# One layer-pair step of a hybrid recurrent decoder on one Trainium2 core: where the small weights and the mask table lie in SBUF, and when they are loaded

## The chip, the cores and the metric

The kernel runs on one core of one Trainium2 chip. The metric is the device time of one launch in microseconds (us), the median over several runs. The engines are TensorE (PE, with its weight loads PEld), VectorE (DVE), ScalarE (ACT), GpSimd (POOL) and SyncE (SP), which issues nearly all DMA transfers in the order of its queue.

## What is computed

A trunk of two layers runs over 592 tokens at once: 16 meta tokens, 8 sample sequences of 8 tokens and a prompt of 512. The width is 1024. Layer 0 ("even") has Mamba-2 SSD heads beside RG-LRU blocks, layer 1 ("odd") has GLA heads beside HGRN2 heads. Cut to what matters:

```python
for layer in range(2):
    mixed = _even_mixer(h, ...) if layer == 0 else _odd_mixer(h, ...)
    h = _layer_norm(ALPHA * h + mixed, ln1_g[layer], ln1_b[layer])
    h = _layer_norm(ALPHA * h + square(relu(h @ w1[layer])) @ w2[layer], ln2_g[layer], ln2_b[layer])

# even mixer: one narrow input (dt, 16 columns) beside the wide ones
z, xbc, dt_raw, rg_gate, rg_x = jnp.split(h @ w_in_even, EVEN_SPLIT, -1)
# odd mixer: one narrow input (lrg, 16 columns) beside the wide ones
qg, kg, vg, gg, lrg, qh, fh, ih, gh = jnp.split(h @ w_in_odd, ODD_SPLIT, -1)
```

The two narrow inputs, `dt_raw` and `lrg`, are the "small" products: 1024 x 16 weights each.

## The kernel before

**Tiling.** Tokens lie along the free dimension, features on 128 partitions; an activation is 8 tiles H[0..7] of 128 x 592. Each fp32 value is held as two fp32r parts (high and remainder), so that a product of a 1024 x 128 weight unit takes 8 x 3 matmuls for each half of the tokens (296 columns a half). The line of these matmuls is L183; L196 holds the mlp's products, L260 the small product of the even mixer, and L324 the products in `together`, where several outputs take turns over k = 0..7, so that the matmuls of k need H[k] alone.

**Weights.** Units of 512 KB come in the order of use: `load_unit` (L121, SP, three buffers), then `parts` makes the two parts on ACT (L127) and DVE (L128) into one of five buffers.

**The small weights and the masks.** `masks(stack, layer)` opens a pool at the start of each mixer, loads the mask table `msk` (128 x 1122, L103), then the small weights (L106), and splits those on ACT and DVE (L107, L108) into `wsr`. SP reads its queue in order, so the load at L106 stands behind that at L103.

**Places in SBUF.** Pools are stacked: a pool that is opened takes the space that the closed ones before it left, and each of its tiles waits for the readers and writers of those old tiles that it lies over. Worked out from the tile shapes in the order of the pools (a pool's first tile takes the lowest slot, the next ones go down from the top), the masks of the first mixer lie over the tiles of the first loads of x and over the scratch of `softplus` and of the gate table (L411 to L422); the masks of the second mixer lie over the tiles rs[0] and rs[7] of the first layer's mlp.

**Start.** `prep_to(1)`, the first half of x, `prep_to(2)`, the vector table `vec`, the second half of x (L365, split at L347 and L348). The first products are `conv[0]`, the small product and `conv[1]`, each for the first half and then for the second (`by_half`).

**Between the layers.** The first mlp ends with the products of w2 for the second half, the norm's sums (L508, L510), and `finishing`, which makes H for the next layer in L539 (DVE), L540 (ACT) and L541 (DVE). After that POOL adds the bias to rs[0..7] (L756) and writes them to DRAM with its own DMAs (L757, `keep`), as the residual of the next layer. The odd mixer starts with `together(ts[:4], 0)`: the small product, q, k and v0 for the first half; then v1; then the second half. An output is copied out of PSUM (L1510 for the small product, L1495 for q, k and v) into a tile of the pool `go`; there are five PSUM buffers for products.

**Order.** A planner lays down each engine's order of instructions at build time from its own estimates of when operands are ready, earlier lines of the program first; on the chip each engine then keeps that order.

Of the kernel before, what the change touches and what calls it, by code (L numbers as in the profile page):

```python
# [8 lines left out]
F32 = mybir.dt.float32  # L9
F32R = mybir.dt.float32r  # L10
I32 = mybir.dt.int32
AF = mybir.ActivationFunctionType
OP = mybir.AluOpType

P = 128
D = 1024
KT = 8
# [23 lines left out]
FULL = ((0, CS), (CS, T))  # L41
# [7 lines left out]
VEC = {}  # L49
_n = 0  # L50
for _name, _w in (("cw", 80), ("cb", 20), ("ssdg", 8), ("dskip", 8), ("ba", 8), ("bx", 8), ("lam", 8),
# [2 lines left out]
    VEC[_name] = _n  # L54
    _n += _w
NVEC = _n

MSK = {}
_n = 0
# [4 lines left out]
NMSK = _n  # L64
# [7 lines left out]
def _trunk(ctx, tc, nc, I, O):  # L72
    V, A, G, PE = nc.vector, nc.scalar, nc.gpsimd, nc.tensor

    def pool(name, bufs=1, stack=ctx, **k):
        return stack.enter_context(tc.tile_pool(name=name, bufs=bufs, reuse_waits="tile", **k))

    const = pool("const")
# [9 lines left out]
    def px():  # L88
        return pxp.tile([P, 512], F32, tag="px", name="px")

    vec = const.tile([P, NVEC], F32, name="vec")
    row = const.tile([P, 32], F32, name="row")
    ones = const.tile([P, P], F32, name="ones")

    def vc(name, i=0, n=1):
        o = VEC[name] + i
        return vec[:, o:o + n]

    def masks(stack, layer):

        sp = pool("mskp", stack=stack)
        t = sp.tile([P, NMSK], F32, name="msk")
        nc.sync.dma_start(t, I["msk"])  # L103
        small = sp.tile([P, KT, 32], F32R, name="wsr")
        r = sp.tile([P, KT, 16], F32, name="wsm")
        nc.sync.dma_start(r, I["wsm"][:, layer])  # L106
        A.copy(small[:, :, 0:16], r)  # L107
        V.tensor_tensor(small[:, :, 16:32], r, small[:, :, 0:16].bitcast(F32), OP.subtract)  # L108
        return lambda name: small if name == "small" else t[:, slice(*MSK[name])]

# [52 lines left out]
    def prep_to(n):  # L165
        while state["next"] < min(n, len(items)):
            u = state["next"]
            state["next"] += 1
            prepped[u] = items[u]()
# [164 lines left out]
    def run(tasks, by_half=False, after=None):  # L334
        if by_half:
            for i in range(2):
                for t in tasks:
                    t.half(i)
                if after:
                    after(i)  # L340
        else:
            for t in tasks:
                t.half(0)
                t.half(1)
# [8 lines left out]
    def new_h():  # L353
        return [act_tile(hp, "h") for _ in range(KT)]


    H = new_h()
    prep_to(1)
    with ExitStack() as st:
        xt = pool("xp", KT, stack=st)  # L360
        xs = [xt.tile([P, T], F32, tag="xt", name="xt") for _ in range(KT)]

        def load(c0, c1):
            for k in range(KT):
                nc.sync.dma_start(xs[k][:, c0:c1], I["x"][:, k, c0:c1])  # L365
                split(H[k], xs[k], c0, c1)

        load(*FULL[0])
        prep_to(2)
        nc.sync.dma_start(vec, I["vec"])  # L370
        load(*FULL[1])
    nc.sync.dma_start(row, I["row"])
    G.memset(ones, 1.0)

# [14 lines left out]
        G.tensor_scalar(m, x, 0.0, None, OP.max)  # L389
        V.scalar_tensor_tensor(out, t, 2.0, m, OP.mult, OP.add)  # L390

    hcw = const.tile([P, 48], F32, name="hcw")
    hcb = const.tile([P, 12], F32, name="hcb")
    hb = const.tile([P, 16], F32, name="hb")
    sp4 = const.tile([P, 8], F32, name="sp4")
    hg = const.tile([P, 3], F32, name="hg")
    lbt = const.tile([P, 3, 8], F32, name="lbt")
    nlam = const.tile([P, 8], F32, name="nlam")
    V.tensor_scalar(hcw, vc("cw", 0, 48), 0.5, None, OP.mult)
    V.tensor_scalar(hcb, vc("cb", 0, 12), 0.5, None, OP.mult)  # L400
    V.tensor_scalar(hb, vc("ba", 0, 16), 0.5, None, OP.mult)
# [143 lines left out]
    def out_proj(g, ys, close, res, halves, layer):  # L545

        c0, c1 = halves[0][0], halves[1][1]
        out = [None]
        with ExitStack() as st:
            rs, m1, m2 = {}, new_h(), []  # L550
            for k in range(KT):
                split(m1[k], ys[k], c0, c1)

            def first(j):
                rs[j] = g("r")
                nc.sync.dma_start(rs[j][:, c0:c1], res[:, j, c0:c1])

                def f(p, a, b, i):
                    V.scalar_tensor_tensor(rs[j][:, a:b], rs[j][:, a:b], ALPHA, p, OP.mult, OP.add)
                return Task(m1, halves, f)  # L560

            def second(j):
                def f(p, a, b, i):
                    V.tensor_tensor(rs[j][:, a:b], rs[j][:, a:b], p, OP.add)  # L564
                    if j >= KS:
                        norm.add(j, i)
                return Task(m2, halves, f)

            def after(i):
                if out[0] is None:  # L570
                    out[0] = new_h()
                norm.finish(i, out[0])

            for j in range(KT):
                run([first(j)])
                if j == JW:
                    drain()
                    close()
                    ap = pool("oact", KT, stack=st)
                if j >= JW:  # L580
                    while len(m2) < min(KT, (j - JW + 1) * -(-KT // (KT - JW))):
                        k = len(m2)
                        m2.append(act_tile(ap, "m2"))
                        split(m2[k], ys[KT + k], c0, c1)
            norm = Norm(g, rs, halves, "ln1g", "ln1b", layer)
            run([second(j) for j in range(KS)])
            norm.shift()
            run([second(j) for j in range(KS, KT)], by_half=True, after=after)
        return out[0]


    def mlp(H, layer, halves, last, keep=None):

# [4 lines left out]
        with ExitStack() as st:  # L598
# [26 lines left out]
            def operands(i):  # L625

                for k in (i, i + 4):
                    h = H[k][:, :, c0:c1].bitcast(F32)
                    V.tensor_tensor(rs[k][:, c0:c1], h[:, 0], h[:, 1], OP.add)
# [9 lines left out]
            def last_operand(i):  # L639

                t2 = turned[i][:, :, 2, :n].bitcast(F32)
                b21 = H[i + 4][:, :, lo].bitcast(F32)
                t4 = H[i][:, :, hi]
                x = stage()[:, 0, :n]
# [145 lines left out]
    def even_mixer(H, g, mk):  # L790
        ident, umask, lsmask, uxmask, lxmask, seqm, sel, blk = (
            mk(n) for n in ("ident", "u", "ls", "ux", "lx", "seq", "sel", "blk"))
        st = ExitStack()
        cp = pool("cp", 2, stack=st)
        sm = pool("sm", 1, stack=st)
# [319 lines left out]
        ys = [None] * 16  # L1115
        conv = []
        for i, key in ((8, ("B", 0)), (10, ("C", 0)), (9, ("B", 1)), (11, ("C", 1))):
            grp[key] = g("bc")
            conv.append(ssd_conv(i, grp[key], lambda: None))
        run([conv[0], Task(H, FULL, dt_consume, small=mk("small")), conv[1]], by_half=True)  # L1120
        run(conv[2:3])
        active.append(group(0))
        run(conv[3:4])
# [121 lines left out]

    def odd_mixer(H, g, mk):
        ident, umask, lsmask, uxmask, lxmask, seqm, sel, blk = (
            mk(n) for n in ("ident", "u", "ls", "ux", "lx", "seq", "sel", "blk"))  # L1250
        st = ExitStack()
        sm = pool("osm", 1, stack=st)
        sd = pool("osd", 1, stack=st)
        wg2 = sm.tile([32, 512], F32, name="wg2")
        nc.sync.dma_start(wg2, I["wg2"])
        rmask = sm.tile([P, T], F32, name="rmask")
# [248 lines left out]
        ys = []  # L1505
# [23 lines left out]
        for h in range(4):  # L1529
            q, k, v0, v1 = (g(n) for n in ("q", "k", "v", "v"))  # L1530
            tasks = [copy_task(q, TAIL), copy_task(k, FULL), copy_task(v0, FULL), copy_task(v1, FULL)]
            if h == 0:
                ts = [Task(H, FULL, lr_consume, small=mk("small"))] + tasks
                together(ts[:4], 0)
                ts[4].half(0)
                together(ts[:2], 1)
                together(ts[2:4], 1)
                ts[4].half(1)
            else:
                run(tasks)  # L1540
            z = [g("zs"), g("zs")]
            while len(lsg) <= h:
                weave()
            active.append(attend(q, k, lsg[h], 1.0 / 16, P ** -0.5, (v0, v1), z, hg[:, 0:2],
                                 I["gst"][h], O["gla_s"][h], O["gla_p"][h], 1))
            run([silu_task(z[0]), silu_task(z[1])])
# [17 lines left out]
        for h in range(8):  # L1564
# [4 lines left out]
            ls, k = fk[h]  # L1569
# [5 lines left out]
        return ys, st.close  # L1575

    with ExitStack() as st:
        mk = masks(st, 0)
        gp = pool("ge", NGE, stack=st)

        def g(name="g"):
            return gp.tile([P, T], F32, tag="g", name=name)

        ys, close = even_mixer(H, g, mk)
        H = out_proj(g, ys, close, I["x"], FULL, 0)
    res = tc.dram_tile([P, KT, T], F32, name="res")
    H = mlp(H, 0, FULL, False, keep=res)
    with ExitStack() as st:
        mk = masks(st, 1)
        gp = pool("go", NGO, stack=st)  # L1590

        def g(name="g"):
            return gp.tile([P, T], F32, tag="g", name=name)

        ys, close = odd_mixer(H, g, mk)
        ln_set.append(True)
        H = out_proj(g, ys, close, res, EVEN_TAIL, 1)
    mlp(H, 1, EVEN_TAIL, True)
# [157 lines left out]
```

## Time and profile before

| | us |
|---|---|
| median of 3 runs | 1940.32 (1939.97 to 1941.08) |
| the profiled execution | 1940.13 |
| its span | 1938.4 |
| PE busy | 1820.5 |
| DVE, ACT, POOL busy | 1411.8, 1020.7, 370.2 |

The span runs from the first to the last instruction; 1.7 us of the profiled execution's time lie around it. "Busy" is the sum over an engine's instructions. Times in the views are microseconds from the start of the span. The chain of waits goes back from the last instruction, at each step to what released it.

### The profile page before, as it was taken

To read this page: it belongs to the slowest core of one execution; us is meant where nothing else is said; L and a number is where in the kernel's file an instruction comes from. 1 tells how busy PE (TensorE), PEld (TensorE's weight loads), DVE (VectorE), ACT (ScalarE), POOL (GpSimd) and SP (SyncE) were. 2 spreads that over 40 slices of the span, in tenths; PEclk is the share of its full clock that TensorE was granted. 3 is DMA by queue.
4 is the path that set the end of the run, shared out by engine and by line. 5 is a ranking of instruction groups with operands and counts; after the bars stand their busy time and mean duration, and the time that the engine had idled before them with its cause. 6 is when DMAs were issued, how large, how long until landed. Compare 5 with 4: busy or idle time off the path is not lost.

```text
span 1938.4 us, 33527 instructions
## 1 busy us (share of the span) xinstructions
PE 1820.5 (94%) x13534; PEld 1766.0 (91%) x13534; DVE 1411.8 (73%) x2332; ACT 1020.7 (53%) x1903; POOL 370.2 (19%) x403
## 2 busy tenths in 40 slices
PE   4999999999999999992999999999999899999997
PEld 4998999898999999991899999999999899999996
DVE  4767766868999898866345557656565999989868
ACT  3656556623646474623354456566552464646443
POOL 0222232215100000256012222212111400000025
PEclk7999999999999999996899999999999999999998
DMA  5232321421122322313123232332332113232221
GB/s 191 71 109 72 108 96 50 133 89 55 57 71 91 99 87 88 109 66 136 57 101 112 101 101 78 100 102 89 101 127 77 55 55 99 77 109 80 95 98 49
DMA packets 69050, 176.53 MB, mean 91 GB/s; under 512 B 6656, under 2 KB 30464, under 8 KB 67744
## 3 DMA queue, kind: packets, MB, share of 16 engines
q1 hardware_dynamic: 68256, 171.97, 27.1%
q8 instruction: 106, 1.74, 0.4%
q0 software_dynamic: 640, 2.43, 0.3%
q14 instruction: 48, 0.39, 0.1%
HBM read 155.12 MB, written 19.25 MB: 90 GB/s over the span
## 4 chain that ended last, share of the span: by engine, by line
PE 68%; DVE 17%; ACT 6%; issue 4%; POOL 2%; DMA 2%; SPq 0%; ACTq 0%; DVEq 0%; POOLq 0%
PE pm L183 37%; PE pm L196 18%; PE pm L324 3%; DVE w L128 3%; ACT w L127 2%; DVE r L523 1%; POOL sq L675 1%; DVE r L459 1%; PE px L1455 1%; DVE h L541 1%; DVE r L539 1%; POOL r L756 1%; ACT sq L671 1%; DVE acc L824 1%; PE px L1466 1%
## 5 line engine op out<-in xcount | busy, mean ns | idle before, releaser
L183 PE MATMUL pm<-h,w 128*128 128x296 f32 (+2 forms) x5424 | 790.6, 302 | 6.4 <-ACT h L347 5.8
L183 PEld LDWEIGHTS pm<-h,w 128*128 128x128 f32 x5424 | 746.8, 189 | 16.7 <-ACT h L347 5.8
L128 DVE TENSOR_TENSOR w<-raw,w 128x1024 fp32r<-128x1024 f32 x348 | 412.1, 1186 | 136.5 <-ACT w L127 134.6
L127 ACT CAST w<-raw 128x1024 fp32r<-128x1024 f32 x348 | 342.8, 989 | 311.6 <-PE pm L183 110.6
L196 PE MATMUL pm<-ff,w 128*128 128x296 f32 (+1 forms) x2016 | 285.1, 299 | 6.3 <-ACT w L127 3.1
L196 PEld LDWEIGHTS pm<-ff,w 128*128 128x128 f32 x2016 | 273.7, 188 | 15.6 <-ACT w L127 5.5
L196 PE MATMUL pm<-h,w 128*128 128x296 f32 (+1 forms) x1152 | 166.1, 298 | 1.8 <-DVE sq L724 0.9
L196 PEld LDWEIGHTS pm<-h,w 128*128 128x128 f32 x1152 | 158.0, 188 | 4.6 <-ACT sq L727 2.4
L675 POOL TENSOR_TENSOR sq<-sq 128x296 f32<-128x296 f32 (+1 forms) x32 | 27.7, 866 | 636.5 <-ACT ff L674 634.4
L196 PE MATMUL pm<-t,w 128*128 128x296 f32 (+1 forms) x864 | 124.5, 297 | 1.0 <-ACT sq L727 0.7
L196 PEld LDWEIGHTS pm<-t,w 128*128 128x128 f32 x864 | 118.5, 188 | 1.7 <-ACT sq L727 1.2
L183 PE MATMUL pm<-ff,w 128*128 128x296 f32 (+1 forms) x768 | 105.9, 298 | 0.9 <-DVE ff L676 0.9
L183 PEld LDWEIGHTS pm<-ff,w 128*128 128x128 f32 x768 | 103.7, 188 | 2.1 <-DVE ff L676 1.4
L183 PE MATMUL pm<-m,w 128*128 128x296 f32 (+1 forms) x768 | 105.2, 298 | 0.0
L183 PEld LDWEIGHTS pm<-m,w 128*128 128x128 f32 x768 | 103.9, 188 | 0.4
L324 PE MATMUL pm<-h,w 128*128 128x296 f32 (+1 forms) x528 | 81.7, 311 | 9.4 <-DVE r L564 6.7
L324 PEld LDWEIGHTS pm<-h,w 128*128 128x128 f32 x528 | 77.0, 198 | 12.2 <-ACT h L540 7.3
L736 DVE TENSOR_TENSOR r<-r,pm 128x296 f32<-128x296 f32 (+1 forms) x168 | 74.9, 452 | 11.2 <-PE pm L196 10.5
L622 ACT CAST ff<-sq 128x296 fp32r<-128x296 f32 (+5 forms) x96 | 58.0, 618 | 24.4 <-DVE sq L692 11.6
L623 DVE TENSOR_TENSOR ff<-sq,ff 128x296 fp32r<-128x296 f32 (+5 forms) x96 | 64.4, 685 | 5.1 <-ACT ff L622 4.5
L1490 POOL TENSOR_TENSOR o<-o,zs 128x576 f32<-128x576 f32 x16 | 30.8, 1935 | 151.7 <-DVE o L1489 151.7
L1409 POOL TENSOR_TENSOR sin<-sin,ebl 128x1024 f32<-128x1024 f32 (+1 forms) x12 | 31.2, 2600 | 97.9 <-issue 93.2
(410 smaller groups left out, 2502.1 us busy)
## 6 DMA issues: line engine op xcount, KB each, us to landing
raw<-in_w_dram SPq DMA_DIRECT2D x252, 512.0 KB, 3.7
sin<-in_sst_dram SPq DMA_DIRECT2D x8, 512.0 KB, 3.8
out_ssd_s_dram<-sin SPq DMA_DIRECT2D x8, 512.0 KB, 3.6
sin<-in_gst_dram SPq DMA_DIRECT2D x4, 1024.0 KB, 5.8
out_gla_s_dram<-sin SPq DMA_DIRECT2D x4, 1024.0 KB, 3.9
sin<-in_hst_dram SPq DMA_DIRECT2D x8, 512.0 KB, 4.6
out_hgrn_s_dram<-sin SPq DMA_DIRECT2D x8, 512.0 KB, 3.5
xt<-in_x_dram SPq DMA_DIRECT2D x16, 148.0 KB, 3.7
```

The source lines that it names most:

```text
L127: A.copy(w[:, 0, :n], r)
L128: V.tensor_tensor(w[:, 1, :n], r, w[:, 0, :n].bitcast(F32), OP.subtract)
L183: PE.matmul(p[:, :n], w[:, a, ks], xs[k][:, b, c0:c1], start=(k == 0 and i == 0), stop=(k == KT - 1 and i == 2))
L196: PE.matmul(p[:, :n], w[:, a, ks], xs[k][:, b, :n], start=(first and k == 0 and i == 0), stop=(k == 3 and i == 2), skip_group_check=True)
L324: PE.matmul(o[:, :c1 - c0], w, t.xs[k][:, b, c0:c1], start=(k == 0 and j == 0), stop=(k == KT - 1 and j == len(ops) - 1))
L459: V.tensor_tensor(rs[k][:, c0:c1], rs[k][:, c0:c1], c[:, c0:c1], OP.subtract)
L622: A.copy(t[:, 0], x)
L623: V.tensor_tensor(t[:, 1], x, t[:, 0].bitcast(F32), OP.subtract)
L675: G.tensor_tensor(x, x, x, OP.mult)
L736: return lambda p: V.tensor_tensor(y, y, p, op)
L1409: G.tensor_tensor(sin, sin, ebl[:, 0:8].unsqueeze(2).to_broadcast([P, 8, N]), OP.mult)
L1490: G.tensor_tensor(o[v][:, c], o[v][:, c], gate[v][:, c], OP.mult)
```

## The change

The small weights of both mixers are loaded in one transfer (`wsm`, 128 KB) right after the first half of x and split at once: the even mixer's into `wse`, the odd mixer's into `wsr`, which is moved to the pool that lives for the whole kernel. A new pool `evc` is opened ahead of x and closed after the even mixer: it holds `wse`, the first mixer's masks, the columns of the vector table that only the even mixer reads, `row` and five small tables. So those tiles have space of their own, and the load of the first mixer's masks is written right behind the second half of x. The vector table is loaded in two pieces. The odd mixer's masks are now loaded in `odd_mixer` into its pool `osm`, behind the 26 tiles of `go`; the pool `mskp` is gone, and `go` starts 6 KB lower.

```diff
--- before.py
+++ after.py
@@ -54,6 +54,7 @@
     VEC[_name] = _n
     _n += _w
 NVEC = _n
+NEVEN = VEC["ln1g"]
 
 MSK = {}
 _n = 0
@@ -88,25 +89,19 @@
     def px():
         return pxp.tile([P, 512], F32, tag="px", name="px")
 
-    vec = const.tile([P, NVEC], F32, name="vec")
-    row = const.tile([P, 32], F32, name="row")
+    vec = const.tile([P, NVEC - NEVEN], F32, name="vec")
+    wsr = const.tile([P, KT, 32], F32R, name="wsr")
     ones = const.tile([P, P], F32, name="ones")
 
     def vc(name, i=0, n=1):
         o = VEC[name] + i
-        return vec[:, o:o + n]
-
-    def masks(stack, layer):
-
-        sp = pool("mskp", stack=stack)
-        t = sp.tile([P, NMSK], F32, name="msk")
-        nc.sync.dma_start(t, I["msk"])
-        small = sp.tile([P, KT, 32], F32R, name="wsr")
-        r = sp.tile([P, KT, 16], F32, name="wsm")
-        nc.sync.dma_start(r, I["wsm"][:, layer])
-        A.copy(small[:, :, 0:16], r)
-        V.tensor_tensor(small[:, :, 16:32], r, small[:, :, 0:16].bitcast(F32), OP.subtract)
-        return lambda name: small if name == "small" else t[:, slice(*MSK[name])]
+        return even["vec"][:, o:o + n] if o < NEVEN else vec[:, o - NEVEN:o - NEVEN + n]
+
+    def masks(pl, dma):
+
+        t = pl.tile([P, NMSK], F32, name="msk")
+        dma(t, I["msk"])
+        return lambda name: t[:, slice(*MSK[name])]
 
 
 
@@ -356,6 +351,12 @@
 
     H = new_h()
     prep_to(1)
+
+    est = ExitStack()
+    evp = pool("evc", stack=est)
+    even = {"vec": evp.tile([P, NEVEN], F32, name="evec")}
+    row = evp.tile([P, 32], F32, name="row")
+    wse = evp.tile([P, KT, 32], F32R, name="wse")
     with ExitStack() as st:
         xt = pool("xp", KT, stack=st)
         xs = [xt.tile([P, T], F32, tag="xt", name="xt") for _ in range(KT)]
@@ -366,9 +367,16 @@
                 split(H[k], xs[k], c0, c1)
 
         load(*FULL[0])
+        wsm = pool("wsmp", stack=st).tile([P, 2, KT, 16], F32, name="wsm")
+        nc.sync.dma_start(wsm, I["wsm"])
+        for i, w in enumerate((wse, wsr)):
+            A.copy(w[:, :, 0:16], wsm[:, i])
+            V.tensor_tensor(w[:, :, 16:32], wsm[:, i], w[:, :, 0:16].bitcast(F32), OP.subtract)
         prep_to(2)
-        nc.sync.dma_start(vec, I["vec"])
+        nc.sync.dma_start(even["vec"], I["vec"][:, 0:NEVEN])
+        nc.sync.dma_start(vec, I["vec"][:, NEVEN:])
         load(*FULL[1])
+    mk0 = masks(evp, nc.sync.dma_start)
     nc.sync.dma_start(row, I["row"])
     G.memset(ones, 1.0)
 
@@ -389,13 +397,13 @@
         G.tensor_scalar(m, x, 0.0, None, OP.max)
         V.scalar_tensor_tensor(out, t, 2.0, m, OP.mult, OP.add)
 
-    hcw = const.tile([P, 48], F32, name="hcw")
-    hcb = const.tile([P, 12], F32, name="hcb")
-    hb = const.tile([P, 16], F32, name="hb")
-    sp4 = const.tile([P, 8], F32, name="sp4")
+    hcw = evp.tile([P, 48], F32, name="hcw")
+    hcb = evp.tile([P, 12], F32, name="hcb")
+    hb = evp.tile([P, 16], F32, name="hb")
+    sp4 = evp.tile([P, 8], F32, name="sp4")
     hg = const.tile([P, 3], F32, name="hg")
     lbt = const.tile([P, 3, 8], F32, name="lbt")
-    nlam = const.tile([P, 8], F32, name="nlam")
+    nlam = evp.tile([P, 8], F32, name="nlam")
     V.tensor_scalar(hcw, vc("cw", 0, 48), 0.5, None, OP.mult)
     V.tensor_scalar(hcb, vc("cb", 0, 12), 0.5, None, OP.mult)
     V.tensor_scalar(hb, vc("ba", 0, 16), 0.5, None, OP.mult)
@@ -1117,7 +1125,7 @@
         for i, key in ((8, ("B", 0)), (10, ("C", 0)), (9, ("B", 1)), (11, ("C", 1))):
             grp[key] = g("bc")
             conv.append(ssd_conv(i, grp[key], lambda: None))
-        run([conv[0], Task(H, FULL, dt_consume, small=mk("small")), conv[1]], by_half=True)
+        run([conv[0], Task(H, FULL, dt_consume, small=wse), conv[1]], by_half=True)
         run(conv[2:3])
         active.append(group(0))
         run(conv[3:4])
@@ -1245,12 +1253,13 @@
 
 
 
-    def odd_mixer(H, g, mk):
-        ident, umask, lsmask, uxmask, lxmask, seqm, sel, blk = (
-            mk(n) for n in ("ident", "u", "ls", "ux", "lx", "seq", "sel", "blk"))
+    def odd_mixer(H, g):
         st = ExitStack()
         sm = pool("osm", 1, stack=st)
         sd = pool("osd", 1, stack=st)
+        mk = masks(sm, nc.sync.dma_start)
+        ident, umask, lsmask, uxmask, lxmask, seqm, sel, blk = (
+            mk(n) for n in ("ident", "u", "ls", "ux", "lx", "seq", "sel", "blk"))
         wg2 = sm.tile([32, 512], F32, name="wg2")
         nc.sync.dma_start(wg2, I["wg2"])
         rmask = sm.tile([P, T], F32, name="rmask")
@@ -1530,7 +1539,7 @@
             q, k, v0, v1 = (g(n) for n in ("q", "k", "v", "v"))
             tasks = [copy_task(q, TAIL), copy_task(k, FULL), copy_task(v0, FULL), copy_task(v1, FULL)]
             if h == 0:
-                ts = [Task(H, FULL, lr_consume, small=mk("small"))] + tasks
+                ts = [Task(H, FULL, lr_consume, small=wsr)] + tasks
                 together(ts[:4], 0)
                 ts[4].half(0)
                 together(ts[:2], 1)
@@ -1575,24 +1584,23 @@
         return ys, st.close
 
     with ExitStack() as st:
-        mk = masks(st, 0)
         gp = pool("ge", NGE, stack=st)
 
         def g(name="g"):
             return gp.tile([P, T], F32, tag="g", name=name)
 
-        ys, close = even_mixer(H, g, mk)
+        ys, close = even_mixer(H, g, mk0)
         H = out_proj(g, ys, close, I["x"], FULL, 0)
+    est.close()
     res = tc.dram_tile([P, KT, T], F32, name="res")
     H = mlp(H, 0, FULL, False, keep=res)
     with ExitStack() as st:
-        mk = masks(st, 1)
         gp = pool("go", NGO, stack=st)
 
         def g(name="g"):
             return gp.tile([P, T], F32, tag="g", name=name)
 
-        ys, close = odd_mixer(H, g, mk)
+        ys, close = odd_mixer(H, g)
         ln_set.append(True)
         H = out_proj(g, ys, close, res, EVEN_TAIL, 1)
     mlp(H, 1, EVEN_TAIL, True)
```

## Rows read from the trace of the kernel before

**Rows 1.** The page's busy times: engine, busy us, share, instructions.

```profile
PE 1820.5 (94%) x13534; PEld 1766.0 (91%) x13534; DVE 1411.8 (73%) x2332; ACT 1020.7 (53%) x1903; POOL 370.2 (19%) x403
```

**Rows 2.** PE's waits, whole span: waiting line, releaser, us in total, times, longest.

```profile
PE pm L324 <- DVE wsr L108: 33.2, 1, 33.2
PE pm L260 <- DVE wsr L108: 18.7, 1, 18.7
```

**Rows 3.** The chain of waits, first 60 us: start, us, what.

```profile
25.30 0.21 DVE lm L417
26.25 4.47 DMA msk<-in_msk_dram
```

**Rows 4.** Timeline of the start: start, us, engine, line, operation, tiles, count, idle before.

```profile
7.06 6.03 PE L183 MATMUL pm<-h,w 128*128 128x296 f32 x23 [0.68 <-DVE h L348]
...
15.34 0.46 DVE L348 TENSOR_TENSOR h<-xt,h 128x296 fp32r<-128x296 f32 x1
...
18.65 1.23 DVE L128 TENSOR_TENSOR w<-raw,w 128x1024 fp32r<-128x1024 f32 x1 [2.78 <-ACT w L127]
...
31.82 4.16 PE L260 MATMUL pm<-h,wsr 128*32 128x296 f32 x16 [18.72 <-DVE wsr L108]
...
42.81 2.32 PE L260 MATMUL pm<-h,wsr 128*32 128x296 f32 x16
...
44.97 3.44 PE L183 MATMUL pm<-h,w 128*128 128x296 f32 x24
```

**Rows 5.** Stretches of the start (busy by engine, clock, DMA); then its matmuls by shape.

```profile
0.00:13.10 13.10, 6.64 (x24) 5.97 (x24) 6.30 (x14) 7.65 (x15) 0.71 (x8) 1.00 0.87 278
13.10:31.80 18.70, 0.00 (x0) 0.00 (x0) 9.60 (x35) 6.46 (x17) 2.55 (x8) 0.59 0.82 272
31.80:36.00 4.20, 4.18 (x17) 3.04 (x18) 0.00 (x0) 0.00 (x0) 0.00 (x0) 0.50 0.00 0
...
L183 PE MATMUL pm<-h,w 128*128 128x296 f32 x24 | 6.6, 465 | 6.4 <-ACT h L347 5.8 <-DVE h L348 0.7
```

**Rows 6.** The chain of waits between the layers, 860 to 960 us.

```profile
898.37 4.49 POOL r L756 x2
902.85 1.28 POOL res L757 x2
...
917.56 2.82 DMA res<-r
...
925.18 14.58 PE pm L324 x88
```

**Rows 7.** Timeline between the layers, 862 to 960 us.

```profile
867.36 13.80 PE L183 MATMUL pm<-ff,w 128*128 128x296 f32 x99
...
880.40 0.42 SPq L1255 DMA_DIRECT2D wg<-in_wg_dram  x1
...
890.63 1.35 PE L510 MATMUL px<-ln,ones 128*128 128x296 f32 x2
...
903.64 1.70 DVE L541 SCALAR_TENSOR_TENSOR h<-r,vec,h 128x296 fp32r<-128x296 f32 x2 [0.17 <-ACT h L540]
...
938.98 0.40 ACT L1495 COPY q<-pm 128x280 f32<-128x280 f32 x1
...
942.90 0.43 PE L324 MATMUL pm<-h,wsr 128*32 128x296 f32 x2
```

**Rows 8.** Timeline of layer 0's passage from out_proj to the mlp, PE.

```profile
465.91 13.91 PE L183 MATMUL pm<-m,w 128*128 128x296 f32 x99
...
502.04 4.23 PE L324 MATMUL pm<-h,w 128*128 128x296 f32 x29 [1.28 <-ACT sq L671]
```

**Rows 9.** DMA issues by line, whole span: KB each, median us to landing.

```profile
vec<-in_vec_dram SPq DMA_DIRECT2D x1, 113.5 KB, 5.1
```

**Rows 10.** Timeline of layer 1's passage from out_proj to the mlp.

```profile
1547.47 0.39 ACT L671 ACTIVATE sq<-pm 128x288 f32<-128x288 f32 x1
...
1548.21 0.93 DVE L539 SCALAR_TENSOR_TENSOR r<-r,vec,lnr 128x288 f32<-128x288 f32 x2
```

## Prediction

> **What bounds the kernel now.** The page first: PE is busy for 94% of the span [rows 1], so what can be won is PE's idle time, 118 us, and only where PE itself is held. The view of PE's waits then shows two single waits far above the rest, 33.2 and 18.7 us, both for L108, the split of the small weights [rows 2]. Together they are 51.9 us. The next question is what makes L108 late, and the chain of waits answers it for each place.
>
> At the start the chain goes from the last steps on the scratch of the gate table (L417 is one) to the load of the masks, issued at 26.25 and 4.47 us long [rows 3]. The masks lie over that scratch, and the load of the small weights stands behind theirs in SP's queue. PE had finished its first products at 13.09 and goes on at 31.82 [rows 4].
>
> Between the layers the chain runs through POOL: L756 from 898.37, the writes of L757 in pairs, the last one landing at 917.56 + 2.82 = 920.38; then the same two loads, and PE starts at 925.18 [rows 6]. H itself was complete at 905.34, and the products of w2 had ended at 881.16 [rows 7]. PE waited for 128 KB of weights that no step of the layer before touches.
>
> **The change at the start.** The small weights get space of their own and are loaded behind the first half of x; the masks follow the second half. What took PE's time from 31.82 to 48.41, the small product, conv[1] and the second halves, is 16.59 us [rows 4]. Its first 16 matmuls took 4.16 us, the same 16 later 2.32.
>
> Will they run at the full clock when they follow at 13.09? The stretch up to 13.10 shows a granted clock of 1.00, but its 24 matmuls took 465 ns each, against 24 in 3.44 us (143 ns of PE's time each) later: spans overlap, yet 23 of them filled 6.03 us, 262 ns each, the lower of the two levels (1.2 and 2.4 GHz) [rows 4, 5]. The stretch in which PE then stood idle has a mean of 0.59, between 0.50 and 1.00, and the one after it 0.50 throughout [rows 5]: the full level was granted around the end of the first products and lost while PE had nothing to do. With no gap PE should keep it.
>
> The Trainium skill ("TensorE: Matmul & The Clock Gate", Part 1: The HAM clock gate) says that the throttled level is the default and that activity releases it, and that the ramp is too small and too variable to be modelled. By the first half of this the 1.00 at the start is no measurement, as the durations say too; by the second the gain would be put at the bare wait, and the start would give 18.7 instead of 20.6 us, so the sum would be 1885.8.
>
> So I take 16.59 - 4.16 + 2.32 = 14.75 us from 13.09, which ends at 27.84 instead of 48.41: **20.6 us saved**, 18.7 if the clock is not kept.
>
> What could hold PE there instead. The split small weights must be there at 13.09: their load is issued at about 5 us; the vector table, of like size and issued then, landed in 5.1 us [rows 9], so they land at about 10.5, with two copies and two subtractions after it, each shorter than a piece of x (0.46) [rows 4], ready at about 11.5. The margin is 1.6 us. The second half of x, split by 15.80 [rows 4], comes perhaps 1.5 us later, for two more issues on SP, 64 KB more before it and under 1 us more on ACT and DVE; it is wanted after the small product and conv[1]'s first half, at 13.09 + 2.32 + 3.44 = 18.85, so this costs nothing; without that cover it would cost the 1.5 us. The masks, 561 KB, now go ahead of the weight units 2 to 4. At the 272 to 278 GB/s of these stretches [rows 5] that is 2.1 us. Unit 2 was split by 19.88 [rows 4], will be by about 22.5, and is wanted at 27.8: hidden. The chain through the gate table stays, off PE's path.
>
> **The change between the layers.** The small weights are ready since the start, and the masks lie where the mlp's `ff` tiles were, as the GLA gate weights (`wg2`) did, which were issued at 880.40 without holding SP [rows 7]. Three things are late next.
>
> First, PE's own work. `together(ts[:4], 0)` can follow the last product of w2 at 881.16, k by k as H's first half is finished, while the norm of the second half runs. Layer 0's passage into the mlp has that form without a small product: from the last product of out_proj at 479.82 to the first one of the second half at 502.04 are 22.2 us, with 96 matmuls in it [rows 8]. Here there are 88 and then 24 for v1, 16 more, 2.3 us: 881.16 + 24.5 = 905.7. If the planner instead leaves all of it behind the norm's sums, which end at 891.98, the 17.72 us that the first half took (925.18 to 942.90) end at 909.7 [rows 6, 7].
>
> Second, H: complete at 905.34 [rows 7], perhaps 1 us later with PE busy when the sums come.
>
> Third, a wait that the change adds. With `go` 6 KB lower, its first tile, q of the first head, lies exactly over rs[0]; before, it lay over rs[3] and rs[6]. So the copy of q's first half (L1495, ACT) waits until rs[0] is written out: the first pair of writes starts at 902.85 [rows 6], and with 2.82 us the first lands at 905.7; the copy takes 0.40 [rows 7], and q's second half, which takes the same PSUM buffer after four others, can start at 906.1. Behind that copy on ACT stand the other copies, and whatever steps of L540 the planner puts there; the second half of H needs those, about 1 us.
>
> The three meet at 905.3 to 907; I take 906.5. Before, the second half began at 942.90 [rows 7]: **36.4 us saved**, 37.6 at best, 33.2 if the first half stays behind the sums. After that the order of work is the same as before; POOL is through its writes when the first head needs it.
>
> **Small terms.** In layer 1's mlp the first tile of squares now lies over three other tiles of `go`, one of which held the norm's scale in the kernel before. Its last reader, L539, ends at 1549.14, and the first write (L671) came at 1547.47 [rows 10]: 0 to 1.7 us lost, since the tiles may fall otherwise; I take 0.8. In layer 0 the same pairs of tiles overlap as before. The splits and loads that go from between the layers save nothing more.
>
> **The sum.** The profiled execution took 1940.13, its span 1938.4; the median of the runs is 1940.32, so nothing is to be corrected. 1940.13 - 20.6 - 36.4 + 0.8 = 1883.9, forecast **1884.0**. With its own bounds (18.7 and 33.2 at the low end, 20.6 and 37.6 at the high end, 0 to 1.7): 1882 to 1890; with what I can't see, 1879 to 1891.
>
> **Rivals.**
>
> *The place of q frees late.* If an early output of `together` comes to lie under one of the tiles that POOL writes last, the wait goes to 920.38, as the masks' did [rows 6]. Then the second half starts at about 921.0, and 21.9 us instead of 36.4 are saved: 1898.4. For it: eight tiles of `go` lie over rs[0..7]. Against: q takes the first slot, and the next ones go down from the top, far from rs.
>
> *The start's wait only moves.* If the planner sets the small weights behind the second half of x, they can be split only after 15.80 [rows 4], about 16.5; PE waits 3.4 us and may lose the clock (1.8): 1887.3 to 1889.1. The order of the lines speaks against it.
>
> *The gain between the layers doesn't come.* If something else that together needs is late, a new wait would take the whole of it: 1919.5. No wait of PE there names anything but L108 [rows 2].
>
> *Slower.* SP keeps its order, so if the planner puts the masks' load of the second mixer early among the weight loads of the mlp, all units behind it wait until `ff` is free at 881.16. Three loaded and five split units of 48 matmuls at 143 ns [rows 4] cover 55 us of such a hold; from 55 + 56 = 111 us on the kernel gets slower than before, one for one: held for 120 us it would take 1949. Against it: `wg2`, with the same wait, held nothing [rows 7].
>
> **How the numbers follow.** Forecast 0.70, with no-fill and a lost clock in it; place of q 0.12; start 0.07; no gain between the layers 0.05; slower 0.03; still faster than 1879, 0.03. Forecast and start alone hold 0.77, so the range reaches up to the place of q: 1879 to 1899. A difference of 0.2%, 3.9 us, is about what a measurement of this kernel tells from none. Faster 0.95, same 0.02, slower 0.03.
>
> **What would show it.** In the profile after: no wait of PE for L108; conv[1]'s second half ended at about 28; matmuls of L324 between 881 and 905 on the old scale; the second half of the small product about 57 us earlier than before, at 886; ACT's L1495 for q held by the DMA of rs[0]. The prediction is wrong if PE shows an idle time of over 5 us at either place, or if later stages, the same as before in my sum, grow.

## The result, and the profile after

| | before | after |
|---|---|---|
| median, us | 1940.62 | 1880.79 |
| runs | 1939.97 to 1941.08 | 1879.81 to 1884.34 |
| profiled execution | 1940.13 | 1884.34 |
| its span | 1938.4 | 1882.5 |

The ratio is 0.9695 (95% interval 0.9678 to 0.9712): 59.8 us or 3.1% faster. The forecast was 1884.0. (The kernel before has four runs here, and three in the table ahead.)

The page of the changed kernel has the same work on PE in a shorter span, and the view of PE's waits no longer names the split of the small weights (L374 now). The two waits of [rows 2] are gone, and no wait is longer than the one for the first data.

```profile
PE 1820.3 (97%) x13534; PEld 1767.0 (94%) x13534; DVE 1411.5 (75%) x2332; ACT 1019.3 (54%) x1903; POOL 369.7 (20%) x403
```

PE's waits over the whole span of the changed kernel:

```profile
PE pm L319 <- DVE r L572: 6.5, 4, 1.8
PE pm L178 <- ACT h L342: 6.0, 1, 6.0
PE px L516 <- DVE ln L487: 4.4, 3, 1.6
```

**The start.** The timeline of the changed kernel, where L178 is the old L183, L255 the old L260 and L862 the first use of the masks by PE:

```profile
7.27 4.91 PE L178 MATMUL pm<-h,w 128*128 128x296 f32 x23 [0.68 <-DVE h L343]
...
9.77 0.28 DVE L374 TENSOR_TENSOR wse<-wsm,wse 128x128 fp32r<-128x128 f32 x1
...
12.01 2.30 PE L255 MATMUL pm<-h,wse 128*32 128x296 f32 x16
...
14.14 6.70 PE L178 MATMUL pm<-h,w 128*128 128x296 f32 x48
...
20.68 2.31 PE L255 MATMUL pm<-h,wse 128*32 128x296 f32 x16
...
22.83 3.42 PE L178 MATMUL pm<-h,w 128*128 128x296 f32 x24
...
26.17 1.28 PE L862 MATMUL px<-msk,dtf 32*128 32x16 f32 x10
```

PE goes from the first products into the small product without a gap. The weights were split at 10.05, 2.0 us before PE wanted them. The small product's first 16 matmuls take 2.30 us where they took 4.16 [rows 4]: PE kept the higher clock (granted clock 1.00 from 12.0 to 14.3). conv[1]'s second half ends at 22.83 + 3.42 = 26.25 instead of 48.41, **22.2 us earlier**.

**Between the layers.** The timeline of the changed kernel, where L319 is the old L324, L1519 the copy of the small product, L1504 the copies of q, k and v, and L1333 the first head's first transposes:

```profile
847.63 13.80 PE L178 MATMUL pm<-ff,w 128*128 128x296 f32 x99
...
860.67 0.42 SPq L103 DMA_DIRECT2D msk<-in_msk_dram  x1
...
861.27 0.43 PE L319 MATMUL pm<-h,wsr 128*32 128x296 f32 x2
...
883.19 2.52 PE L319 MATMUL pm<-h,wsr 128*32 128x296 f32 x15
...
883.58 1.33 POOL L765 DMA_DIRECT2D res<-r  x2
...
886.55 0.39 ACT L1519 COPY lgf<-pm 32x296 f32<-32x296 f32 x1 [1.72 <-PE pm L319]
887.13 3.51 PE L319 MATMUL pm<-h,w 128*128 128x296 f32 x24
...
890.68 1.04 ACT L122 CAST w<-raw 128x1024 fp32r<-128x1024 f32 x1 [3.74 <-PE pm L319]
891.64 0.38 ACT L1504 COPY q<-pm 128x280 f32<-128x280 f32 x1
...
892.07 6.80 PE L319 MATMUL pm<-h,w 128*128 128x296 f32 x48 [0.24 <-ACT q L1504]
...
912.01 1.04 PE L1333 MATMUL px<-msk,v 128*128 128x128 f32 x8
```

The last product of w2 ends at 861.43, and the small product for the first half follows at 861.27 (matmuls overlap at their ends). The masks are loaded at 860.67. From that last product to the first transposes PE needs 50.6 us. Before, it needed 88.9: from 881.16 [rows 7] to 970.06, by the same line of the old trace. That is **38.3 us saved**.

It is more than the 33.2 us of the wait for the weights. The kernel before also stood still until the norm's sums could start; here PE works on the next layer in that time. PE's waits of this kind over the whole span, before (the 8.0 us stand at this place):

```profile
PE px L508 <- DVE ln L479: 12.5, 4, 8.0
```

In the changed kernel the longest of them is 1.6 (L516 above). New short waits for the parts of H as they are finished, 3.8 us in two and 0.5, take part of it back.

**The rest.** Both traces hold the same work from 48.41 (26.25) to 881.16 (861.43) and from 970.06 (912.01) to the end. The first stretch became 2.4 us longer, the second 2.2 us. So the spans differ by 22.2 + 38.3 - 2.4 - 2.2 = 55.9 us, while the medians differ by 59.8. What these 4.6 us are comes last in the experiments.

### The profile page after: what moved, and what is told of

It is laid out like the page before. It is cut to its first block, busy times and chain, and to the rows that moved or that the text cites. A ratio compares the mean times of both kernels' runs of the same rounds, so it can differ in the third digit from the quotient of the medians.

```text
span 1882.5 us, 33533 instructions
## 1 busy us (share of the span) xinstructions
PE 1820.3 (97%) x13534; PEld 1767.0 (94%) x13534; DVE 1411.5 (75%) x2332; ACT 1019.3 (54%) x1903; POOL 369.7 (20%) x403
## 4 chain that ended last, share of the span: by engine, by line
PE 70%; DVE 17%; ACT 7%; issue 4%; POOL 1%; DMA 1%; ACTq 0%; DVEq 0%; POOLq 0%
PE pm L178 38%; PE pm L191 19%; DVE w L123 3%; PE pm L319 3%; ACT w L122 2%; DVE r L531 1%; POOL sq L683 1%; DVE r L467 1%; DVE r L547 1%; PE px L1464 1%; DVE h L549 1%; ACT sq L679 1%; PE px L1202 1%; PE px L1475 1%; PE px L1474 1%
## 5 line engine op out<-in xcount | busy, mean ns | idle before, releaser
L178 PE MATMUL pm<-h,w 128*128 128x296 f32 (+2 forms) x5424 | 790.2, 302 | 6.7 <-ACT h L342 6.0
L178 PEld LDWEIGHTS pm<-h,w 128*128 128x128 f32 x5424 | 746.6, 189 | 16.7 <-ACT h L342 6.0
L178 PE MATMUL pm<-ff,w 128*128 128x296 f32 (+1 forms) x768 | 106.0, 298 | 0.9 <-DVE ff L684 0.9
L178 PEld LDWEIGHTS pm<-ff,w 128*128 128x128 f32 x768 | 103.7, 188 | 2.1 <-DVE ff L684 1.4
L178 PE MATMUL pm<-m,w 128*128 128x296 f32 (+1 forms) x768 | 104.9, 298 | 0.0
L178 PEld LDWEIGHTS pm<-m,w 128*128 128x128 f32 x768 | 103.6, 188 | 0.4
L319 PE MATMUL pm<-h,w 128*128 128x296 f32 (+1 forms) x528 | 83.6, 316 | 13.1 <-DVE r L572 6.5
L319 PEld LDWEIGHTS pm<-h,w 128*128 128x128 f32 x528 | 78.0, 202 | 17.4 <-ACT h L548 11.6
```

The source lines that it names most:

```text
L178: PE.matmul(p[:, :n], w[:, a, ks], xs[k][:, b, c0:c1], start=(k == 0 and i == 0), stop=(k == KT - 1 and i == 2))
L319: PE.matmul(o[:, :c1 - c0], w, t.xs[k][:, b, c0:c1], start=(k == 0 and j == 0), stop=(k == KT - 1 and j == len(ops) - 1))
```

## The experiments

The figures are medians beside runs of the kernel before on the same chip; the ratio is to those. The two kernels with one gain each, the one with the first mixer's masks in their old place and the one with 2400 bytes left unused ran together, the other three on another occasion. The changed kernel ran again with those three, at 1882.48 us, ratio 0.9692 (0.9679 to 0.9705); kernels of the first occasion are compared with it by the ratios.

**The two gains apart.** The first kernel changes the start alone, the second the place between the layers alone. The first one's edit to the changed kernel:

```diff
-    wsr = const.tile([P, KT, 32], F32R, name="wsr")
...
+    def masks_small(stack):
+        sp = pool("mskp", stack=stack)
+        mk = masks(sp, nc.sync.dma_start)
+        small = sp.tile([P, KT, 32], F32R, name="wsr")
+        r = sp.tile([P, KT, 16], F32, name="wsm")
+        nc.sync.dma_start(r, I["wsm"][:, 1])
+        A.copy(small[:, :, 0:16], r)
+        V.tensor_tensor(small[:, :, 16:32], r, small[:, :, 0:16].bitcast(F32), OP.subtract)
+        return lambda name: small if name == "small" else mk(name)
...
+        mk1 = masks_small(st)
         gp = pool("go", NGO, stack=st)
```

> The start as in the changed kernel; the odd mixer opens a pool ahead of its tiles again, loads its masks and then its own small weights there. Theory (two waits for small weights, each with its own price, which add up): the 22 us of the start stay and the wait of about 33 us between the layers comes back, so 1940.6 - 22 = about 1918.5 us (1916 to 1921). Rival (one gain needs the other, for instance because the stretch up to the second layer is limited by the weight loads and gives back what the start wins): clearly above 1925 us, or below 1912 us if part of the gain between the layers has another cause than the small weights.

Measured: 1920.12 us (1918.83 to 1921.30), ratio 0.9887 (0.9869 to 0.9904), 21.3 us faster than before.

The second one's edit: the same function, with the even mixer's weights, called ahead of that mixer's tiles, and `mk0` and `wse` taken out of `evc`:

```diff
-    wse = evp.tile([P, KT, 32], F32R, name="wse")
...
-    mk0 = masks(evp, nc.sync.dma_start)
...
+        mk0 = masks_small(st)
         gp = pool("ge", NGE, stack=st)
```

> The odd mixer as in the changed kernel, its small weights split during the first loads; the even mixer loads its masks and then its small weights in a pool of its own behind the scratch of the gate table, as before. Theory: the wait of 18.7 us at the start comes back with the half clock after it, the 38 us between the layers stay: 1940.6 - 38 = about 1902.5 us (1900 to 1906). With the run before it, the two gains should add up to the 59.8 us of the whole change within 4 us. Rival: they don't add up (a sum below 52 us or above 66 us).

Measured: 1904.20 us (1903.20 to 1905.01), ratio 0.9805 (0.9791 to 0.9820), 37.2 us faster than before.

PE's longest wait in the first kernel, then in the second:

```profile
PE pm L328 <- DVE wsr L112: 33.0, 1, 33.0
```

```profile
PE pm L265 <- DVE wse L113: 21.7, 1, 21.7
```

Each kernel keeps one of the two waits, and the gains add up: 21.3 + 37.2 = 58.5 against 59.8, a difference that the runs can't tell from none. Neither gain needs the other, and the weight loads between the two places give nothing back. The second kernel's wait is longer than the 18.7 us of before, since its masks go out at 27.87 instead of 26.25 and its first products end 0.7 us earlier; its conv[1] (L188 is the old L183) ends at 50.15, 1.7 us later than before:

```profile
27.87 0.33 SPq L103 DMA_DIRECT2D msk<-in_msk_dram  x1
```

```profile
46.73 3.42 PE L188 MATMUL pm<-h,w 128*128 128x296 f32 x24
```

**Is it the small weights or the masks, at the start?** The masks go back behind the scratch of the gate table, the small weights stay early:

```diff
-    mk0 = masks(evp, nc.sync.dma_start)
...
+        mk0 = masks(pool("mskp", stack=st), nc.sync.dma_start)
         gp = pool("ge", NGE, stack=st)
```

> The changed kernel, but the first mixer's mask table is loaded in a pool of its own behind the scratch of the gate table, as before; only the small weights come early. Theory (both are needed: the masks are first used by PE right after the first products, at about 26 us, and their load can't start before the scratch is free at about 30 us and takes 4.5 us): 4 to 9 us slower than the changed kernel, 1885 to 1890 us. Rival (only the small weights count, the planner puts other products ahead of the masks' first use): no difference, 1880 to 1882 us.

Measured: 1883.72 us (1882.59 to 1888.21), ratio 0.9704 (0.9686 to 0.9723). The timeline of this kernel's start (L861 is the first use of the masks here):

```profile
22.75 13.53 PE L178 MATMUL pm<-h,w 128*128 128x296 f32 x98
...
37.24 1.28 PE L861 MATMUL px<-msk,dtf 32*128 32x16 f32 x10 [0.97 <-DMA msk<-in_msk_dram]
```

```profile
33.54 0.33 SPq L103 DMA_DIRECT2D msk<-in_msk_dram  x1
```

The masks are issued at 33.54 and PE feels 0.97 us of it. The planner put the first use of the masks behind the 48 products of conv[2] and 26 of conv[3]'s. The medians against the changed kernel's ratio, 0.9704 to 0.9692, make some 2 us, with intervals that overlap and are too wide to rule out 4; the trace shows 1, and the span of the profiled execution is 1880.8, as that of the changed kernel in its second profile. By the trace my 4 to 9 us are refuted. At the start nearly the whole gain is the small weights'.

**The small weights behind the second half of x.** The second half of x and what is loaded with it are written ahead of the load and the split of the small weights:

```diff
         load(*FULL[0])
+        prep_to(2)
+        nc.sync.dma_start(even["vec"], I["vec"][:, 0:NEVEN])
+        nc.sync.dma_start(vec, I["vec"][:, NEVEN:])
+        load(*FULL[1])
         wsm = pool("wsmp", stack=st).tile([P, 2, KT, 16], F32, name="wsm")
         nc.sync.dma_start(wsm, I["wsm"])
...
-        prep_to(2)
-        nc.sync.dma_start(even["vec"], I["vec"][:, 0:NEVEN])
-        nc.sync.dma_start(vec, I["vec"][:, NEVEN:])
-        load(*FULL[1])
```

> The changed kernel with the load and the split of the small weights put behind the second half of x. The prediction's rival for the start: the weights are split at about 16.5 us, PE stands still from about 12.5 until then, 3.4 to 5.5 us slower than the changed kernel: 1884 to 1886.5 us. Rival of that, after the run with the masks in their old place, where the planner moved other products ahead: it puts conv[1]'s first half ahead of the small product and nothing is lost, 1880 to 1882 us.

Measured: 1889.61 us (1887.80 to 1892.03), ratio 0.9730 (0.9717 to 0.9743), some 7 us slower than the changed kernel at 1882.48 beside it. The span of the profiled execution is 1886.0 against 1880.8, 5.2 us. Its timeline at the start:

```profile
11.51 0.43 SPq L375 DMA_DIRECT2D wsm<-in_wsm_dram  x1
...
16.07 3.37 PE L255 MATMUL pm<-h,wse 128*32 128x296 f32 x16 [4.20 <-DVE wse L378]
19.24 7.25 PE L178 MATMUL pm<-h,w 128*128 128x296 f32 x48
```

PE waits 4.20 us, the 16 matmuls take 3.37 instead of 2.30 and the 48 behind them 7.25 instead of 6.70, part of them at the lower clock (granted 0.52 and 0.50 from 17 to 19.5): 5.8 us together. The profile is that of the fastest of the four executions, so the 7 us of the medians are not all seen in it. This is the mechanism that the prediction named as a rival for the start. Here the planner did not move conv[1] ahead, as it had moved conv[2] in the kernel with the old masks.

**The place of q between the layers.** 2400 bytes left unused push q of the first head from rs[0], written out first, over rs[7], written out last:

```diff
+        pad = pool("gpad", 1, stack=st).tile([P, 600], F32, name="gpad")
+        G.memset(pad[:, 0:1], 0.0)
         gp = pool("go", NGO, stack=st)
```

> The changed kernel with 2400 bytes a partition left unused ahead of the odd mixer's tiles, so that q of the first head lies over rs[7] and rs[3] instead of rs[0]; rs[7] is written out last, at about 902 on the changed kernel's scale. The prediction's step (q's second half needs the PSUM buffer of q's first half, and so the copy into that place): the second half starts about 14.5 us later, so 1895 us (1892 to 1898). Rival, from the trace of the changed kernel (q's second half takes the buffer that the small product left, and the copy of q stands behind other work on ACT anyway): only two of five PSUM buffers are held for longer, 0 to 4 us lost, 1880 to 1885 us.

Measured: 1892.16 us (1891.75 to 1893.87), ratio 0.9745 (0.9731 to 0.9760), some 10 us slower than the changed kernel by the ratios. The timeline of this kernel between the layers:

```profile
885.40 3.52 PE L319 MATMUL pm<-h,w 128*128 128x296 f32 x24
...
899.48 0.39 ACT L1504 COPY q<-pm 128x280 f32<-128x280 f32 x1 [9.48 <-DMA res<-r]
...
899.77 0.41 ACT L1504 COPY k<-pm 128x296 f32<-128x296 f32 x1
899.92 8.29 PE L319 MATMUL pm<-h,w 128*128 128x296 f32 x48 [9.82 <-ACT q L1504]
```

The copy of q waits 9.48 us for the write of rs[7], the copies of k and v stand behind it on ACT and show no wait of their own, and PE waits 9.82 us for a PSUM buffer. The 48 matmuls after that wait take 8.29 us where they took 6.80 in the changed kernel: the granted clock is 0.53 from 899.9 to 903.4. Both expectations were half right: q's own second half ran at 885.40, in the buffer that the small product left, but one task later PE needs a buffer and finds none, because ACT keeps its order. What keeps this wait out of the changed kernel is that its q lies over rs[0].

**The masks of the second mixer in their old place.** They lie ahead of `go` again; the small weights stay early. q then lies over rs[7] and rs[3], as in the kernel just shown:

```diff
-        mk = masks(sm, nc.sync.dma_start)
...
+        mk1 = masks(pool("mskp", stack=st), nc.sync.dma_start)
         gp = pool("go", NGO, stack=st)
```

> The changed kernel with the second mixer's masks in a pool of their own ahead of the odd mixer's tiles again, so over rs[0] and rs[7], while the small weights stay early. q of the first head then lies over rs[7] and rs[3], as in the run with 2400 bytes left unused. Theory (the masks' load and its wait on SP cost nothing by themselves, only the place of q does): within 2 us of that run, 1890 to 1894 us. Rival (SP is held by the masks' load until about 902 us, and the weight units behind it come late): slower by another 3 us or more, 1895 to 1905 us.

Measured: 1893.89 us (1891.09 to 1895.48), ratio 0.9751 (0.9738 to 0.9764), the same as with the unused bytes. ACT's copy of q in this kernel, and then SP's queue:

```profile
899.29 0.39 ACT L1503 COPY q<-pm 128x280 f32<-128x280 f32 x1 [9.51 <-DMA res<-r]
```

```profile
899.29 0.33 SPq L103 DMA_DIRECT2D msk<-in_msk_dram  x1
899.73 30.27 SPq L116 DMA_DIRECT2D raw<-in_w_dram  x5
```

The masks' load holds SP until 899.29 and the weight units behind it go out after it, and that adds nothing to the wait for q. What costs about 11 us is the place of q again. Since PE waits for q until the same time, this doesn't show what the hold of SP would cost by itself.

**Is any of that wait left in the changed kernel?** v1, the last of the four outputs in each half, takes the place over rs[0]:

```diff
-            q, k, v0, v1 = (g(n) for n in ("q", "k", "v", "v"))
+            v1, q, k, v0 = (g(n) for n in ("v", "q", "k", "v"))
```

> The changed kernel with the order of the first head's tiles changed to v1, q, k, v0, so that v1 and not q takes the place over rs[0]. Theory (in the changed kernel rs[0] is written out before ACT comes to the copy of q, PE waited 0.2 us for it): no difference, 1880 to 1882 us. Rival (the wait for rs[0] holds the second half, as the prediction had it): 2 to 5 us faster, 1875 to 1879 us.

Measured: 1883.33 us (1880.31 to 1884.54), ratio 0.9694 (0.9681 to 0.9708), no difference. PE's wait for the copy of q stands as it was:

```profile
PE pm L319 <- ACT q L1504: 0.2, 1, 0.2
```

In the changed kernel rs[0] is written out before ACT comes to the copy: POOL issues the first pair of writes from 883.58 on, and after 887 the DMA engines move nothing more of it, while the copy starts at 891.64. Two stretches of the changed kernel (columns as explained below):

```profile
885.00:887.00 2.00, 1.37 (x6) 0.54 (x5) 1.13 (x2) 0.39 (x1) 2.00 (x2) 1.00 0.76 282
887.00:889.00 2.00, 2.00 (x15) 1.87 (x14) 0.00 (x0) 0.00 (x0) 2.00 (x2) 1.00 0.00 0
```

**The changed kernel again, and the 4.6 us.**

> The changed kernel itself, as the measure for the three beside it: 1880 to 1882 us. In its first profile the time was 1884.3, with the lower clock for 6.8 us near 170 us and again near 1475 us; the other executions were 3 to 4.5 us shorter. If such stretches explain the spread, a shorter execution shows fewer of them.

Measured: 1882.48 us (1880.78 to 1883.93). The profiled executions of the changed kernel here (1882.54 us) and of the one with v1 first (1880.31 us) do the same work at the same times as the first profile (1884.34 us), so three stretches can be laid side by side: 160 to 180, 325 to 340 and 1465 to 1485. Columns: stretch, its length, busy us and count of PE, PEld, DVE, ACT, POOL, then clock, DMA share, GB/s. First the changed kernel's first profile:

```profile
160.00:180.00 20.00, 17.54 (x126) 16.96 (x123) 14.74 (x30) 9.82 (x31) 6.60 (x6) 0.83 0.24 84
...
325.00:340.00 15.00, 12.45 (x75) 11.34 (x74) 11.80 (x20) 7.84 (x17) 5.81 (x11) 0.89 0.36 125
...
1465.00:1485.00 20.00, 16.84 (x99) 15.81 (x99) 17.83 (x34) 8.93 (x18) 5.65 (x6) 0.83 0.24 80
```

Then its second profile:

```profile
160.00:180.00 20.00, 17.41 (x144) 16.64 (x145) 15.01 (x31) 11.13 (x34) 7.17 (x6) 0.91 0.25 84
325.00:340.00 15.00, 12.44 (x84) 11.72 (x83) 12.75 (x19) 7.79 (x18) 5.82 (x11) 1.00 0.38 123
1465.00:1485.00 20.00, 16.71 (x99) 15.67 (x98) 17.84 (x32) 8.99 (x18) 6.79 (x7) 0.83 0.24 77
```

And the one with v1 first:

```profile
160.00:180.00 20.00, 17.55 (x143) 16.80 (x132) 15.29 (x31) 10.61 (x33) 7.17 (x6) 0.91 0.26 84
325.00:340.00 15.00, 12.44 (x73) 11.73 (x72) 11.71 (x17) 7.38 (x15) 5.41 (x10) 0.89 0.30 105
1465.00:1485.00 20.00, 16.68 (x117) 15.59 (x116) 19.91 (x36) 10.03 (x21) 6.82 (x7) 1.00 0.26 81
```

And the kernel before, at the same work:

```profile
180.00:200.00 20.00, 16.93 (x140) 15.91 (x140) 15.05 (x31) 11.36 (x34) 6.31 (x6) 0.91 0.24 88
...
345.00:360.00 15.00, 12.42 (x85) 11.70 (x84) 12.75 (x22) 8.67 (x19) 5.97 (x12) 1.00 0.37 125
...
1525.00:1545.00 20.00, 16.54 (x116) 15.46 (x115) 19.92 (x36) 10.04 (x21) 6.82 (x7) 1.00 0.25 80
```

In each stretch the same program gets a lower mean clock in one execution than in another, and fewer matmuls through: 99 at 0.83 against 117 at 1.00 in the last. The first profile has the lowest clock in all three, alone or level with another, and is the longest. Compared by the starts of the same matmuls, it falls behind the trace of before by 1.6, 1.4 and 2.3 us in the three stretches, and gains 0.8 back between 410 and 460. So the 4.6 us lie, to a few tenths, in these stretches. They belong to the execution, not to the change; what decides whether a stretch gets the higher clock wasn't tried.

## Why the prediction was right, point by point

**What bounds the kernel** held. Both waits were for the small weights, and taking them away gave back all of their 51.9 us and 8 more.

**The total.** The terms were 4.3 us too small together: 1.6 at the start, 1.9 between the layers, and 0.8 for a small term that did not come. That the profiled execution, at 1884.34 us, agrees with the forecast of 1884.0 is luck, since the lower clock cost it 4.6 us; the median is 3.2 us below the forecast.

**The start: 20.6 us forecast, 22.2 in the trace, 21.3 by the kernel that has only this.** The clock was kept, as the rows on it suggested. The 1.9 us between the two versions of the sum were there (2.30 against 4.16 for the same 16 matmuls). The Trainium skill ("TensorE: Matmul & The Clock Gate", Part 1: The HAM clock gate) puts the ramp aside as too small a share of a kernel to model; 1.9 us are 0.1% of this span, which agrees, but nearly a tenth of what this place had to give. The Trainium skill's other statement there, that the lower level is the default and activity releases it, agrees: in the changed kernel four matmuls run in each half microsecond from 8.0 to 10.5, and five or six from 10.5 on.

The term was 1.6 us too small. The 23 matmuls of the start took 4.91 us here and 6.03 before, since the clock rose earlier, and so the first products ended 0.9 us earlier. In the kernel that has the old start they took 4.91 too, so this varies by execution and isn't the change's. The sum also left out that the lower clock of before lasted beyond the 16 matmuls: the 48 behind them took 7.21 us before and 6.70 here. The covers held: weights ready at 10.05 (forecast 11.5), and the second half of x split at 16.26, 0.5 us later than before and not 1.5. Two sizes in the prediction are exchanged: the load that PE waited for had 64 KB, and 128 KB more go ahead of the second half of x.

**Between the layers: 36.4 us forecast, 38.3 in the trace, 37.2 by the kernel that has only this.** q's second half began at 887.13, which is 906.9 on the old scale (19.7 us earlier in all); I had 906.5. The rest is that the planner ran the small product's second half ahead, k by k as H was finished, 16 matmuls or 2.3 us that were then out of the way. The fill while the norm runs came as layer 0's passage had suggested [rows 8].

**The step that was wrong** is how the added wait works. I had q's second half take q's own buffer "after four others". It took the one that the small product left, and the copy of q stood on ACT behind the cast of a weight unit, by which time rs[0] had been written for more than 4 us. So the sign that I had named, ACT's copy of q held by the DMA of rs[0], did not show, and the time was met at another limit: H was complete at 886.13, the small product's last matmul followed at 886.19, and its copy out of PSUM (886.55 to 886.94) freed the buffer that q took at 887.13. The prediction had its three limits within 2 us of each other, so taking the wrong one hardly moved the sum. The wait is real all the same. With q over the last write it costs 9.8 us of PE's time and 1.5 of clock; I had priced that rival at 14.5, since I let the whole second half wait where only what comes after q does.

**The rival for the start** was priced at 3.4 to 5.2 us. It cost 5.2 us by the spans of the profiled executions and some 7 by the medians: the mechanism was right and the price somewhat low.

**Small terms.** The 0.8 us for the first tile of squares did not come. The rows are the kernel before, then the changed one:

```profile
PE pm L324 <- ACT sq L671: 2.8, 2, 1.5
```

```profile
PE pm L319 <- ACT sq L679: 2.5, 2, 1.3
```

**Slower** did not come up: the masks' load went out at 860.67 with `wg2`, behind the weight units. Where the experiment did hold SP, for the old place of the masks, the hold ended with the wait for q and added nothing to it.

**Expected of later runs and wrong:** that the first mixer's masks matter at the start, and that the kernel with the small weights behind x takes at most 1886.5 us (1889.61 measured). The planner works around a late operand where there is other work in line, as with the masks, and didn't where the small product was late.

## What to carry to other kernels

A long wait for a small transfer is often neither the transfer nor its size: ask what its place in memory held before, and what stands ahead of it in its queue. (No run here separates the two for the small weights: they left the queue behind the masks and got a place of their own at once.) Data that depends on nothing can be loaded and prepared at the start if a few KB can be had for the whole kernel. When places move, look at which tile now lies over the one that is freed last, and who first writes there: on an engine that keeps its order, one copy into a place that isn't free holds all that stand behind it, and through their PSUM buffers TensorE.

## What was not expected of the hardware

The share of the higher clock in the same stretch of the same program differs from execution to execution. In stretches where PE has short idle times (83 to 88% busy) the mean granted clock was 0.83, 0.89, 0.91 or 1.00, and one such stretch cost the profiled execution 1.4 to 2.3 us against the trace of before. The four first executions of the changed kernel, 1879.81 to 1884.34 us, go in order of their mean clock over the span, from 0.994 to 0.991. With a change of 60 us this doesn't matter; for one of 3 us it is the noise to count with.
